# A weight set summed apart, and norm factors carried through DRAM, in a one-core decoder layer

## The chip, the core and the metric

The kernel runs on one core of a Trainium2 chip. The core has a matrix engine (TensorE, PE in the profile), a vector engine (VectorE, DVE), a scalar engine (ScalarE, ACT), GpSimd (POOL) and SyncE (SP), which issues transfers. ACT and POOL issue transfers too. PE writes its results to PSUM; the other data live in SBUF (128 partitions) and in DRAM. Each engine works through its own list of instructions in order, and waits on semaphores for the others.

The metric is the time of one execution in microseconds on the device. The kernel before takes 1294.37 us, the median of three runs (1293.19 to 1296.22).

## What is computed

One hybrid decoder layer for 512 tokens of width 1024, all in float32: a SwiGLU FFN, a mixer with two groups of heads side by side, a cross-attention into a memory of 256 rows, a second FFN, and a final norm. Cut to what the change touches:

```python
def rms_norm(x, w):
    y = x32 * lax.rsqrt(jnp.mean(x32 * x32, axis=-1, keepdims=True) + EPS)
    return y.astype(x.dtype) * w

def swiglu(h, w_in, w_out):                     # D_FF = 2816
    gate, up = jnp.split(h @ w_in, 2, axis=-1)
    return (jax.nn.silu(gate) * up) @ w_out

# mixer, state-space heads: 4 groups of 256 channels
    y = y.reshape(bsz, seqlen, SSD_WIDTH) * jax.nn.silu(z.astype(jnp.float32))
    yg = y.reshape(bsz, seqlen, SSD_GROUPS, SSD_WIDTH // SSD_GROUPS)
    yg = yg * lax.rsqrt(jnp.mean(yg * yg, axis=-1, keepdims=True) + EPS)
    y_ssd = yg.reshape(bsz, seqlen, SSD_WIDTH).astype(h.dtype) * ssd_norm_w
# mixer, differential attention: 8 heads of 128 values
    o = diff_attention(q, k, v, lam, rel_bias)
    o = o * lax.rsqrt(jnp.mean(o * o, axis=-1, keepdims=True) + EPS)
    y_attn = (o.astype(h.dtype) * subln_w * (1.0 - lambda_init)).reshape(bsz, seqlen, DA_WIDTH)
    return jnp.concatenate([y_ssd, y_attn], axis=-1) @ w_out
```

So each of the eight attention heads and each of the four groups needs one factor per token: the inverse root of a mean over 128 or 256 channels.

## The kernel before, in words

Activations lie with channels on the partitions and the 512 tokens along the row. A float32 product is made of three matmuls: both operands are split into a high part (rounded to the type fp32r) and a low part (the rest), and high times high, low times high and high times low are summed in PSUM. A split costs a copy on ACT (`wh`, lines 155 and 1314) and a subtraction on DVE (`wl`, lines 156 and 1316). Weights come in tiles of 128 x 1024 (512 KB).

SP and POOL issue their instructions in the order in which the code is written. On PE, DVE and ACT the order is fixed when the kernel is built. A class `Order` mixes the work: dense products run one after the other, and chains of small steps (heads, groups) are resumed when the PE time already written out passes a due time; a table `W` holds the distances. `behind(...)` ties an instruction behind others on its engine.

**Heads.** `head` (line 768) ends with `po`, the head's output (128 channels x 512 tokens) in PSUM. ACT copies it to `of`; PE transposes it in four blocks (`ptk`), so that tokens lie on partitions; ACT squares the blocks and sums each row (`junk`, `ss`); DVE makes `ev`, POOL raises it to the power -1/2 (`rr`, line 858); DVE multiplies (`on`); PE transposes back (`pot`), and ACT and DVE split the result, with the gain `wsub`, into `yah` and `yal`.

**Groups.** `group` (line 930) ends with two tiles `y`. ACT squares them, DVE adds the squares (`ysq`); PE sums over the channels with a column of ones (`pn`, four float32 matmuls, eight records in the trace); DVE scales (`nv`), POOL takes the power (`ncol`, line 367). `row_of` (line 370) turns the four columns into a row on all partitions: two diagonal matrices (`ndiag`, on POOL for groups 0 to 2) and two PE matmuls with ones (`nrow`). DVE multiplies `y` by its gain and `nrow` (line 1034), and splits.

**The FFN's second product** (`out_blocks`, line 1293) uses a scheme of block sums: `oa`, `oe` and `ob` are PSUM tiles, two each, and weight blocks are added to one another before they are multiplied. The third weight set, S2, multiplies `s24` into `ob`; it is the sum of a set that lies in `wr` and of pieces `more`, added by DVE in place in `wr` (`t2`, line 1362). In the last third of the first FFN (`by_dma`), both parts of S2 are summed behind the two first products, split (`wh`, `wl`), and `ob` starts from a copy of `oa` (line 1422). Two small products `prel`, for the position bias, lie there too.

POOL issues beside this the accumulating transfers (`isum`, `wsum`, 512 KB each) that sum the second FFN's weights in DRAM, long ahead.

Of the kernel before, what the change touches and what calls it, by code (L numbers as in the profile page):

```python
# [38 lines left out]
W |= {"g0": 8.28, "gc": 0.75, "gx": 0.92, "gb": 2.59, "gs": 0.51, "gt": 2.0, "gd": 6.9, "gy": 0.38, "gq": 11.8, "gn": 1.5, "gr": 4.4}  # L39
W |= {"c0": 4.97, "cs": 3.0, "ct": 4.82}  # L40
# [60 lines left out]
def body(tc, a, dbg=None):  # L101
# [38 lines left out]
    last, start, last_sum, recent, newest, newest_mm, first_block, sums_low = [], [], [], [], [], [], [], []  # L140
# [22 lines left out]
    def split(s, src, scale=None, half=False, n=T):  # L163
        if half:
            both = s2(s, R32, (P, 2, T // 2))
            hi, lo = both[:, 0], both[:, 1]
        else:
            hi, lo = s2(s + "h", R32, (P, n)), s2(s + "l", R32, (P, n))
        last[:] = [i.ins for i in split_into(hi, lo, src, scale)]
        return hi, lo  # L170
# [34 lines left out]
    def sums_in_steps(b11, b21, b22, b12, pair=None):  # L205
# [12 lines left out]
        s24 = split("s24", s24)  # L218
        lo, hi = slice(0, H), slice(H, T)
# [149 lines left out]

    def row_of(col, nb, first, second, apart):  # L370
# [71 lines left out]
    def ffn_quads(xs, wq, st, nq, made, places, sums=None, fresh=False, prime=None):  # L442

        for q in range(nq):
# [7 lines left out]
            for i in range(2):  # L452
                row = st.row[:, None, i * H : (i + 1) * H].to_broadcast([P, 2, H])
                V.tensor_tensor(gate[:, 2 * i : 2 * i + 2], halves(gs[i]), row, ALU.mult)  # L454
# [8 lines left out]
    def block_tiles(g, n, tied=False):  # L463
# [12 lines left out]
        def made(th):  # L476
            g.append({})
            if len(g) < n:
                od.spawn(steps(th, g[-1], 2.9), 2.9)
            else:  # L480
                with behind(list(recent) if tied else []):
                    for _ in steps(th, g[-1], 0.0):
                        pass
# [125 lines left out]
    dskh = cp.tile([P, 8], F32, name="dskh")  # L609
    rel_d = dram.tile([8, RW], F32, name="rel_d")  # L610

    def lambdas():
# [15 lines left out]
        V.tensor_scalar(dskh, par[:, C_DSKIP : C_DSKIP + 8], 0.5, None, ALU.mult)  # L628

# [138 lines left out]
    def head(hd, q, kq, bias):  # L768
# [75 lines left out]
        of = s2("of")  # L844
        S.activation(of, po, AF.Copy)
# [24 lines left out]
    def out_attn(hg, o0, o1, prep=False):  # L870
# [3 lines left out]
        for o in range(o0, o1):  # L874
            po = acc("pm")
            yield from proj(po, ws.get(o) or load_w(a["woa"][hg, o], 4 * P), heads)
            V.tensor_tensor(x[o], x[o], po, ALU.add)
# [6 lines left out]
    def silu2(src):  # L884
# [3 lines left out]
        V.scalar_tensor_tensor(th, th, 1.0, src, ALU.add, ALU.mult)  # L888
# [41 lines left out]
    def group(g, bt, ct, xs, zs):  # L930
# [93 lines left out]
        yield W["gq"] + (1.2 if g == 2 else 0.0)  # L1024
        pn = aux("pn", (P, 4))
        for b in range(4):
            mm(pn[:, b : b + 1], sq[0][:, b * P : (b + 1) * P], ones[:, 0:1], True, True)

        rh = inv_rms_cols(pn, 4, 4.0 / (4 * 256), 4.0 * EPS)
        yield W["gn"]  # L1030
        pr = yield from row_of(rh, 4, *((G, G) if g < 3 else (V, V)), W["gr"] - (0.8 if g == 3 else 0.0))
# [261 lines left out]
    def out_blocks(blocks, sums, g, col4, ncol4, each=None, finale=None, clean=True, n=None, by_dma=False):  # L1293
# [14 lines left out]
        def weights(of, part, raw=None, low_behind=()):  # L1308
            if raw is None:
                raw = of(part) if callable(of) else fetch(of, part)  # L1310
            w = raw.shape[1]
            hi = wp.tile([P, w], R32, tag="wh", name=nm("wh"))
            lo = wp.tile([P, w], R32, tag="wl", name=nm("wl"))
            high = S.activation(hi, raw, AF.Copy)  # L1314
            with behind(low_behind):
                low = V.tensor_tensor(lo, raw, hi.bitcast(F32), ALU.subtract)  # L1316
            recent[:] = [high.ins, low.ins]
# [44 lines left out]
        def t2(part):  # L1362
            more = pieces.pop(part) if part in pieces else (fetch(blocks[B22], part),)
            n = t_raw[part].shape[1] // len(more)
            for i, m in enumerate(more):
                V.tensor_tensor(t_raw[part][:, i * n : (i + 1) * n], t_raw[part][:, i * n : (i + 1) * n], m, ALU.add)
            return t_raw[part]

# [7 lines left out]
        def t4(part):  # L1376
            G.dma_start(t_raw[part], blocks[B21][:, part[0] * T : part[1] * T], accum_op=ALU.add)

        later, pieces, asked = {}, {}, {}

        def ask_early():
            for of, make in ((B11, lambda part: fetch(blocks[B11], part)), (S1, t1)):
                asked[of, parts[1]] = make(parts[1])
            for part in parts:
                pieces[part] = [s2("more") for _ in range(*part)]
                for k, m in zip(range(*part), pieces[part]):
                    nc.sync.dma_start(m, blocks[B22][:, k * T : (k + 1) * T])
            for part in parts:
                asked[S3, part] = seventh(part)
# [5 lines left out]
        if here:  # L1395
            seventh = added(blocks[B12], blocks[B22], "gate")
            sums = [early_or(S1, t1), early_or(S3, seventh), t2, lambda part: t_raw[part]]
        ready = [None, None]
        if early:
            ready = [{parts[0]: weights(of, parts[0])} for of in (blocks[B11], sums[0])]  # L1400
            yield
        if by_dma:
            ask_early()
# [15 lines left out]
        third = {part: weights(sums[2], part, low_behind=() if n else sums_low) for n, part in enumerate(parts if by_dma else parts[:1])}  # L1419
        third_split = list(recent) if by_dma else []  # L1420
        for t in range(2):
            S.activation(b_ps[t], a_ps[t], AF.Copy)
        with behind(third_split):
# [8 lines left out]
        for n, _ in enumerate(product(a_ps, b21 if here and not by_dma else blocks[B21], "12")):  # L1432
            if n == 12 and by_dma:
                for part in t_raw:
# [190 lines left out]
```

## Time and profile before

| | |
|---|---|
| median of three runs | 1294.37 us (1293.19 to 1296.22) |
| profiled execution, its own time | 1296.8 us |
| its span | 1295.0 us |
| granted PE clock, mean | 0.996 |
| busy | PE 1282.7, DVE 973.5, ACT 707.2, POOL 116.4 us |
| chain that ended last | PE 98%, DVE 1% |

The profiled execution is one that was watched; its own time lies 2.4 us above the median and is the one that the trace's numbers add up to. "PE busy" counts the time in which a matmul is under way; matmuls overlap one another, so the price of a matmul in a dense stretch is the distance between starts. A row of the timeline gives start, duration, engine, line, operation, tiles (written <- read), shape and count, and in brackets the idle time ahead with what ended it. A row of DMA issues gives the queue, the size, and the median time from issue to landing.

### The profile page before, as it was taken

How to read it: one execution, taken by the hardware profiler on the slowest of the kernel's cores; microseconds unless marked ns; L12 is line 12 of the kernel's file. 1: busy time of each engine (PE TensorE's matmuls, PEld its weight loads, DVE VectorE, ACT ScalarE, POOL GpSimd, SP SyncE). 2: the span in 40 equal slices, each digit the busy share in tenths (PEclk: the TensorE clock that was granted, in tenths of full speed). 3: DMA queues.
4: the chain of work that ended last, by engine and by line, in shares of the span. 5: the costliest groups of instructions: out<-in, count | busy, mean ns of one | idle time of the engine just before them, and what ended most of it. 6: DMA issues, size and time to landing. Idle time of an engine off the chain costs nothing.

```text
span 1295.0 us, 20087 instructions
## 1 busy us (share of the span) xinstructions
PE 1282.7 (99%) x7709; PEld 1124.9 (87%) x7709; DVE 973.5 (75%) x1553; ACT 707.2 (55%) x1203; POOL 116.4 (9%) x145
## 2 busy tenths in 40 slices
PE   9999999999999999999999999999999999999997
PEld 7889998998888788877888888889899999989995
DVE  6988898797875776567778697645678878877886
ACT  7545564565654564346644575435466646555554
POOL 1001010001010011100102011020001000000000
PEclk9999999999999999999999999999999999999998
DMA  9368677889874436653475667593249876666662
GB/s 334 97 175 205 181 204 196 226 200 238 260 242 147 139 66 164 225 165 98 106 206 168 175 161 232 190 231 111 66 131 253 212 228 178 191 189 189 184 198 91
DMA packets 69551, 234.75 MB, mean 181 GB/s; under 512 B 8192, under 2 KB 9696, under 8 KB 69104
## 3 DMA queue, kind: packets, MB, share of 16 engines
q1 hardware_dynamic: 53488, 180.91, 42.5%
q0 software_dynamic: 13168, 45.67, 20.0%
q10 hardware_dynamic: 2800, 6.91, 1.6%
q8 instruction: 60, 0.98, 0.3%
q14 instruction: 35, 0.29, 0.1%
HBM read 231.30 MB, written 48.29 MB: 216 GB/s over the span
## 4 chain that ended last, share of the span: by engine, by line
PE 98%; DVE 1%; ACT 0%; issue 0%; POOLq 0%; POOL 0%; ACTq 0%
PE qb L243 13%; PE pm L146 10%; PE qe L243 8%; PE qa L243 8%; PE pxbc L146 7%; PE ob L1328 7%; PE oa L1328 4%; PE oe L1328 4%; PE pk L146 3%; PE pv L146 3%; PE pq L146 3%; PE pcq L146 3%; PE pz L146 3%; PE pck L146 2%; PE pa L146 2%; PE pcv L146 2%
## 5 line engine op out<-in xcount | busy, mean ns | idle before, releaser
L155 ACT ACTIVATE wh<-wr 128x1024 fp32r<-128x1024 f32 (+1 forms) x245 | 251.5, 1028 | 239.0 <-PE qe L243 29.4
L156 DVE TENSOR_TENSOR wl<-wr,wh 128x1024 fp32r<-128x1024 f32 (+1 forms) x245 | 291.1, 1189 | 78.3 <-ACT wh L155 57.8
L1314 ACT ACTIVATE wh<-wr 128x1024 fp32r<-128x1024 f32 (+1 forms) x78 | 77.1, 988 | 71.3 <-PE ob L1328 19.7
L1316 DVE TENSOR_TENSOR wl<-wr,wh 128x1024 fp32r<-128x1024 f32 (+1 forms) x78 | 87.6, 1131 | 15.1 <-ACT wh L1314 12.9
L790 ACT ACTIVATE ec<-ec,mn 128x512 f32<-128x512 f32 (+3 forms) x64 | 35.4, 554 | 21.9 <-DVE mn L789 21.9
L789 DVE CUSTOM_DVE_ANT_0 ec<-ps,bias 128x512 f32<-128x512 f32 (+3 forms) x64 | 28.1, 487 | 15.4 <-PE ps L146 15.3
L252 POOL DMA_DIRECT2D wr<-in_f2q x11 | 9.7, 881 | 308.8 <-DMA wr<-in_f2q 176.3
L367 POOL TENSOR_TENSOR ncol<-nv,mhalf 128x4 f32<-128x4 f32 (+1 forms) x9 | 10.6, 1179 | 295.3 <-DVE nv L365 295.3
L903 DVE SCALAR_TENSOR_TENSOR conv<-pxbc,par,conv 128x511 f32<-128x511 f32 (+2 forms) x48 | 35.8, 745 | 0.6
L146 PE MATMUL pxbc<-hnl,wh 128*128 128x512 f32 x128 | 35.5, 404 | 0.0
L146 PE MATMUL pxbc<-hnh,wh 128*128 128x512 f32 x128 | 34.7, 398 | 0.0
L146 PE MATMUL pxbc<-hnh,wl 128*128 128x512 f32 x128 | 32.5, 393 | 0.0
L454 DVE TENSOR_TENSOR gate<-qb,row 128x512 f32<-128x512 f32 x19 | 13.2, 692 | 22.1 <-PE qb L243 22.1
L146 PEld LDWEIGHTS pxbc<-hnh,wl 128*128 128x128 f32 x128 | 23.7, 188 | 5.2 <-issue 0.2
L252 POOL DMA_DIRECT2D wr<-in_f1q x16 | 14.0, 874 | 151.9 <-DMA wr<-in_f1q 83.0
L146 PEld LDWEIGHTS pxbc<-hnh,wh 128*128 128x128 f32 x128 | 23.3, 189 | 4.6 <-issue 0.3
L146 PEld LDWEIGHTS pxbc<-hnl,wh 128*128 128x128 f32 x128 | 23.2, 188 | 4.7 <-issue 0.4
L455 ACT ACTIVATE gate<-gate 128x1024 f32<-128x1024 f32 x19 | 20.1, 1056 | 10.9 <-DVE gate L454 10.9
L146 PE MATMUL pv<-wh,hnh 128*128 128x512 f32 x64 | 25.3, 396 | 0.0
L146 PE MATMUL pv<-wh,hnl 128*128 128x512 f32 x64 | 25.2, 393 | 0.0
L155 ACT ACTIVATE s24h<-s 128x512 fp32r<-128x512 f32 x30 | 18.8, 626 | 8.1 <-DVE s L214 8.1
L858 POOL TENSOR_TENSOR rr<-ev,mhalf 128x4 f32<-128x4 f32 x8 | 8.3, 1035 | 162.4 <-DVE ev L856 162.4
(465 smaller groups left out, 3548.1 us busy)
## 6 DMA issues: line engine op xcount, KB each, us to landing
wr<-in_f2q SPq DMA_DIRECT2D x44, 512.0 KB, 4.5
wr<-in_f1q SPq DMA_DIRECT2D x40, 512.0 KB, 4.6
wr<-in_f1b SPq DMA_DIRECT2D x23, 512.0 KB, 7.0
isum<-in_f2q SPq DMA_DIRECT2D x22, 512.0 KB, 5.2
wr<-isum SPq DMA_DIRECT2D x22, 512.0 KB, 6.2
wsum<-in_f2b SPq DMA_DIRECT2D x20, 512.0 KB, 6.1
wr<-wsum SPq DMA_DIRECT2D x20, 512.0 KB, 4.7
wr<-in_f1q POOLq DMA_DIRECT2D x16, 512.0 KB, 7.6
```

The costliest lines, as they stand in the source:

```text
L146: newest_mm[:] = [nc.tensor.matmul(out, w, x, start=start, stop=stop).ins]
L155: S.activation(hi, src, AF.Copy),
L156: V.tensor_tensor(lo, src, hi.bitcast(F32), ALU.subtract),
L243: newest_mm[:] = [nc.tensor.matmul(out, w_[:, wc], xs[kp][which][x_], start=first and j == 0 and f == 0 and kp == 0, stop=j == 2 and kp == ...
L252: last_sum[:] = [G.dma_start(raw, m, accum_op=ALU.add).ins]
L455: S.activation(gate, gate, AF.Silu)
L789: V.tensor_tensor_reduce(out=ec[:, :n], in0=ps[c][:, parts[i]], in1=bias[:, T - n :], scale=0.125, scalar=3e38, op0=ALU.add, op1=ALU.min, ...
L790: S.activation(ec[:, :n], ec[:, :n], AF.Exp, bias=mn, scale=-1.0, accum_out=sm[c][:, i : i + 1])
L903: V.scalar_tensor_tensor(y[:, d:], ps[:, : T - d], par[:, cw + j : cw + j + 1], y[:, d:], ALU.mult, ALU.add)
L1314: high = S.activation(hi, raw, AF.Copy)
L1316: low = V.tensor_tensor(lo, raw, hi.bitcast(F32), ALU.subtract)
L1328: newest_mm[:] = [nc.tensor.matmul(ps, a_[:, ts], b_[:, ws], start=first and k == 0 and j == 0, stop=k == n - 1 and j == 2, skip_group_che ...
```

## The change

It has two parts.

**The third set, apart.** In the last third of the first FFN, S2 is no longer summed into `wr` but into the tiles `more` (`t2_apart`). `third_set` does the adds, the splits and the late loads of the first two sets between the steps that split the last FFN tile; the gate's last multiplication is tied behind them. The fourth set is then accumulated onto the `more` tiles, in four transfers of 256 KB in place of two of 512 KB. `weights` is cut into `high` and `low`.

**Factors through DRAM.** For the heads with `hd % 4 < 3` (six of eight) and for groups 0 to 2, tokens no longer go to the partitions through PE. The squares are split, and two matmuls with ones (`ptok`) sum them over the channels, on all partitions; ACT copies one partition of it as a line, already permuted; a transfer on POOL's queue spreads the line over 128 partitions, four tokens on each (`ssum`); POOL adds the epsilon term and takes the power; a transfer writes the 512 numbers to DRAM as one row (`there`), and another reads this row into all partitions (`far`). DVE multiplies it on, tied behind a late neighbour (`near`). Heads 3 and 7 and group 3 stay as they were.

```diff
+W |= {"hn": 4.2, "fs": 7.0, "fw": 6.0, "fr": 9.0}
...
+    def sums_by_token(sq):
+
+        ps = aux("ptok")
+        with behind(list(newest_mm)):
+            for j in range(2):
+                mm(ps, ones_r, sq[j], j == 0, j == 1)
+        line = s2("line")[0:1]
+        S.activation(line.rearrange("o (p b) -> o b p", b=4), ps[0:1].rearrange("o (b p) -> o b p", b=4), AF.Copy)
+        ss = small("ssum", 4, bufs=2)
+        G.dma_start(ss, line.rearrange("o (p b) -> o p b", b=4))
+        return ss
+
+    def row_by_dram(v):
+
+        col = small("fcol", 4, bufs=2)
+        G.tensor_tensor(col, v, mhalf, ALU.pow)
+        there = dram.tile([4, P], F32, name=nm("there"))
+        G.dma_start(bass.AP(there.tensor, there.offset, [[1, P], [P, 4]]), col)
+        yield W["fw"]
+        row = s2("far")
+        G.dma_start(row, bass.AP(there.tensor, there.offset, [[0, P], [1, 4 * P]]))
+        yield W["fr"]
+        return row
...
             for i in range(2):
                 row = st.row[:, None, i * H : (i + 1) * H].to_broadcast([P, 2, H])
-                V.tensor_tensor(gate[:, 2 * i : 2 * i + 2], halves(gs[i]), row, ALU.mult)
+                with behind(recent[2:] if prime and q == nq - 1 and i else []):
+                    V.tensor_tensor(gate[:, 2 * i : 2 * i + 2], halves(gs[i]), row, ALU.mult)
...
+        if hd % 4 < 3:
+            sq = s2("osq")
+            S.activation(sq, po, AF.Square)
+            S.activation(of, po, AF.Copy, scale=wsub_p)
+            sq = split("osq", sq)
+            yield W["hn"]
+            ss = sums_by_token(sq)
+            ev = small("fev", 4, bufs=2)
+            G.tensor_tensor(ev, sm[0], sm[0], ALU.mult)
+            G.tensor_tensor(ev, ev, eps_p, ALU.mult)
+            yield W["fs"]
+            G.tensor_tensor(ev, ev, ss, ALU.add)
+            row = yield from row_by_dram(ev)
+            with behind(list(near)):
+                V.tensor_tensor(of, of, row, ALU.mult)
+            ya[hd] = split("ya", backwards(of))
+            return
...
+        if g < 3:
+            sq = split("ysq", sq[0])
+            yield W["gq"] + (1.2 if g == 2 else 0.0)
+            ss = sums_by_token(sq)
+            v = small("fev", 4, bufs=2)
+            yield W["fs"]
+            G.tensor_tensor(v, ss, eps_g, ALU.add)
+            pr = yield from row_by_dram(v)
...
         for j in range(2):
             n = 2 * g + j
-            V.scalar_tensor_tensor(yz[j], yz[j], par[:, C_SSD + n : C_SSD + n + 1], pr, ALU.mult, ALU.mult)
+            gain = par[:, C_SSD + n : C_SSD + n + 1] if g == 3 else gain_p[:, n : n + 1]
+            with behind(list(near) if g < 3 else []):
+                V.scalar_tensor_tensor(yz[j], yz[j], gain, pr, ALU.mult, ALU.mult)
...
+        def t2_apart(part):
+            for i, m in enumerate(pieces[part]):
+                recent.append(V.tensor_tensor(m, t_raw[part][:, i * T : (i + 1) * T], m, ALU.add).ins)
...
         def ask_early():
+            ask_pieces(parts[0])
             for of, make in ((B11, lambda part: fetch(blocks[B11], part)), (S1, t1)):
                 asked[of, parts[1]] = make(parts[1])
...
+            ask_pieces(parts[1])
+            t2_apart(parts[0])
+            between.append(third_set)
+
+        def third_set():
+            ready[0][parts[1]] = weights(None, parts[1], asked.pop((B11, parts[1])), first_block)
+            with behind(first_block[:1]):
+                w = high(parts[0], pieces[parts[0]])
+            copied_behind[:] = recent
+            with behind(first_block):
+                ready[1][parts[1]] = weights(None, parts[1], asked.pop((S1, parts[1])))
+            with behind(sums_low + recent[1:]):
+                t2_apart(parts[1])
+            third[parts[0]] = low(w)
```

Constants for the new path (`wsub_p`, `gain_p`, `eps_p`, `eps_g`) are made at the start.

How the lists move is shown at three places. The first is the end of the last FFN third on DVE; `more` are the pieces of S2, `wr` the set they are added to. Before:

```order
L454 TENSOR_TENSOR gate_3380<-qb_3135,row_412 128x512
L1316 TENSOR_TENSOR wl_3377<-wr_3373,wh_3376 128x1024
...
L156 TENSOR_TENSOR s31l_3397<-s_597_3391,s31h_3396 128x512
L156 TENSOR_TENSOR s24l_3401<-s_598_3392,s24h_3400 128x512
L156 TENSOR_TENSOR gl_3405<-th_3381,gh_3404 128x512
L1366 TENSOR_TENSOR wr_3373<-wr_3373,more_3413 128x512
L1366 TENSOR_TENSOR wr_3373<-wr_3373,more_3414 128x512
L1366 TENSOR_TENSOR wr_3410<-wr_3410,more_3417 128x512
L1366 TENSOR_TENSOR wr_3410<-wr_3410,more_3418 128x512
```

With the change:

```order
L1443 TENSOR_TENSOR more_3387<-wr_3380,more_3387 128x512
L1443 TENSOR_TENSOR more_3388<-wr_3380,more_3388 128x512
L1392 TENSOR_TENSOR wl_3384<-wr_3380,wh_3383 128x1024
L482 TENSOR_TENSOR gate_3402<-qb_3142,row_415 128x512
...
L157 TENSOR_TENSOR s31l_3419<-s_603_3413,s31h_3418 128x512
L1443 TENSOR_TENSOR more_3396<-wr_3393,more_3396 128x512
L1443 TENSOR_TENSOR more_3397<-wr_3393,more_3397 128x512
L1392 TENSOR_TENSOR wl_3427<-more_3387,wh_3426 128x512
L1392 TENSOR_TENSOR wl_3427<-more_3388,wh_3426 128x512
L157 TENSOR_TENSOR s24l_3439<-s_604_3414,s24h_3438 128x512
L1392 TENSOR_TENSOR wl_3512<-more_3396,wh_3511 128x512
L1392 TENSOR_TENSOR wl_3512<-more_3397,wh_3511 128x512
```

The first part's two adds have gone from behind `gl` to ahead of the last `gate`, and the second part's from there to behind `s31l`.

The second place is the end of head 0 on PE, inside a `pq` product (queries of a later head). Before:

```order
L146 MATMUL pq_4554<-hnl_3919,wh_4557 128x512
L150 MATMUL ptk_4582<-ident,of_4576 128x128 x4
L146 MATMUL pq_4554<-hnl_3947,wh_4557 128x512
L146 MATMUL pq_4554<-hnl_3969,wh_4557 128x512
L146 MATMUL pq_4554<-hnl_3999,wh_4557 128x512
```

With the change:

```order
L147 MATMUL pq_4571<-hnl_4044,wh_4574 128x512
L147 MATMUL ptok_4613<-osqh_4597,ones_r 128x512
L147 MATMUL pq_4571<-hnl_4064,wh_4574 128x512
L147 MATMUL pq_4571<-hnh_3887,wl_4575 128x512
L147 MATMUL ptok_4613<-osql_4598,ones_r 128x512
```

Two matmuls of 512 columns stand near the place where four transposes stood, and the four of `pot` further on are gone.

The third place is group 2, whose last step falls beside the memory's value product (`pcv`, weights `wcv`). On ACT with the change (`ptok` is the group's sum, `btk` the next group's):

```order
L156 ACTIVATE wh_8129<-wr_8127 128x1024
L942 ACTIVATE th_1680_7955<-conv_7931 128x512
L942 ACTIVATE th_1681_7962<-pz_7922 128x512
L156 ACTIVATE wh_8212<-wr_8210 128x1024
L380 ACTIVATE line_8024<-ptok_8021 1x4x128
L1016 ACTIVATE btk_8033<-pbt_8029 128x384
```

On POOL with the change:

```order
L382 DMA ssum_8026<-line_8024 128x1x4
L1355 DMA wsum_288<-in_f2b 128x1024
L1085 TENSOR_TENSOR fev_8028<-ssum_8026,eps_all 128x4
L388 TENSOR_TENSOR fcol_8122<-fev_8028,mhalf 128x4
L390 DMA there_8124<-fcol_8122 128x4x1
L393 DMA far_8167<-there_8124 128x512
L1355 DMA wsum_289<-wsum_287 128x1024 x2
```

And on DVE, from the last multiplication of `gate` to that of `th`, which PE's next `py` reads:

```order
L1050 TENSOR_TENSOR gate_7796<-gate_7796,cbm_7993 128x512
L1099 SCALAR_TENSOR_TENSOR y_7799<-y_7799,gain_p,far_8167 128x512
L157 TENSOR_TENSOR wl_8260<-wr_8257,wh_8259 128x1024
L1065 SCALAR_TENSOR_TENSOR y_8186<-th_1674_7915,dskh,py_8096 128x512
L157 TENSOR_TENSOR wl_8301<-wr_8298,wh_8300 128x1024
L1066 TENSOR_TENSOR y_8186<-y_8186,e_1722_8097 128x384
L1074 TENSOR_TENSOR y_8186<-y_8186,th_1681_7962 128x512
L1050 TENSOR_TENSOR th_7893<-th_7893,cbm_7993 128x512
L1063 SCALAR_TENSOR_TENSOR e_1737_8191<-pf_8267,e_1737_8191 128x384
L157 TENSOR_TENSOR ysl_8248<-y_7799,ysh_8247 128x512
L1050 TENSOR_TENSOR th_7893<-th_7893,cbm_7993 128x512
```

In the old list both multiplications of `y` stood ahead of the row of `gate` that heads this list; now they stand behind it. Between the group's `ssum` and its `fev` POOL issues an accumulate of 512 KB; the two that followed it now follow `far`.

More of the change, by code (lines that the diff above doesn't have):

```diff
@@ L138, in dump @@
             nc.sync.dma_start(dbg[name], t.bitcast(F32) if t.dtype == R32 else t)
[L140 removed]
+    last, start, last_sum, recent, newest, newest_mm, first_block, sums_low, second_high, between, near = ([] for _ in range(11))
     V, S, G = nc.vector, nc.scalar, nc.gpsimd
@@ L1418, in out_blocks @@
         u2 = []
[L1419 to L1423, printed above, removed]
+        if not by_dma:
+            third[parts[0]] = weights(sums[2], parts[0], low_behind=sums_low)
+        with behind(copied_behind + (second_high if by_dma else [])):
+            copied = [S.activation(b_ps[t], a_ps[t], AF.Copy).ins for t in range(2)]
+        if by_dma:
+            with behind(copied):
+                third[parts[1]] = weights(None, parts[1], pieces[parts[1]])
+        with behind(list(recent) if by_dma else []):
             for t in range(2):
```

88 lines of the change are left out of this document (54 added, 34 removed).

## The prediction

> **What bounds the kernel now.** I read the page's busy shares first, then the view of waits of TensorE (PE), then the chain of waits, then the timeline of each place that the change touches.
>
> ```profile
> PE 1282.7 (99%) x7709; PEld 1124.9 (87%) x7709; DVE 973.5 (75%) x1553; ACT 707.2 (55%) x1203; POOL 116.4 (9%) x145
> PE 98%; DVE 1%; ACT 0%; issue 0%; POOLq 0%; POOL 0%; ACTq 0%
> PE ob L1328 <- ACT wh L1314: 1.1, 1, 1.1
> 321.31 5.44 PE oa L1328 x24
> 313.97 7.33 PE ob L1328 x24
> ```
>
> PE is busy 99% of the span, and the chain that ends last is PE for 98%. Twenty-four matmuls of 512 columns take 5.44 us, so one takes 0.227 us start to start. The third row is the one PE wait behind the start, 1.1 us at `ob`; the last shows 24 matmuls behind it that took 7.33 us. So there are two ways to shorten the kernel: fewer PE instructions, and that one stall. VectorE (DVE, 75%), ScalarE (ACT, 55%) and GpSimd (POOL, 9%) count only where they make PE wait.
>
> **First part, the third weight set.** The place is the end of the last third of the first FFN.
>
> ```profile
> 311.48 2.49 DVE L1366 TENSOR_TENSOR wr<-wr,more 128x512 f32<-128x512 f32 x4
> 311.82 1.03 PE L146 MATMUL prel<-hot,rel_sb 32*8 32x256 f32 x4
> 312.86 2.27 ACT L1314 ACTIVATE wh<-wr 128x1024 fp32r<-128x1024 f32 x2 [1.14 <-DVE wr L1366]
> 313.97 1.45 PE L1328 MATMUL ob<-wh,s24h 128*128 128x512 f32 x4 [1.13 <-ACT wh L1314]
> 300.94 0.69 DVE L454 TENSOR_TENSOR gate<-qb,row 128x512 f32<-128x512 f32 x1 [2.80 <-PE qb L243]
> 313.90:318.30 4.40, 4.33 (x12) 3.42 (x13) 4.40 (x7) 3.46 (x7) 2.49 (x3) 0.61 1.00 282
> ```
>
> DVE adds `wr<-wr,more` late, ACT's high copy waits 1.14 us for it, and PE waits 1.13 us for the copy. The last row (busy of PE, PEld, DVE, ACT, POOL, then granted clock, DMA share, GB/s) shows what follows: the clock is 0.61 in these 4.4 us. So the stall costs 1.13 + (7.33 - 5.44 = 1.89) = 3.02 us.
>
> The change puts the adds of the first part into DVE's idle 2.80 us ahead of `gate`, and its high copy on ACT (1.03 us by the row of 77.1 us for 78 would be 0.99) ahead of `s31h`. What is late next is the second part: its adds (two of 0.62), the low copies of the first (two of about 0.65) and `s24l` stand in DVE's order behind `s31l`, which starts at about 309.5; ACT copies `ob` from 310.7 to 311.7. PE leaves the old `oe` at 311.8, and one of the two `prel` products now stands ahead of `ob`, so `ob` finds its inputs some 0.3 to 0.8 us early. I take the whole 3.02; bounds: 1.13 if only the wait goes and the clock drops anyway, 0 if the stall only moves. The `prel` work stays. The accumulates into the third set become four of 256 KB for two of 512 KB, with the same bytes on the same queue; their sums are read by the last of the products, several passes of 5.44 us later, and cost nothing.
>
> **Second part, six heads and three groups.** What leaves PE:
>
> ```profile
> L150 PE MATMUL ptk<-ident,of x32: 272/273/329, 417.3 to 644.4; 128*128 128x128 f32 x32
> L150 PE MATMUL pot<-ident,on x32: 270/272/273, 423.5 to 651.6; 128*128 128x128 f32 x32
> 630.68 0.71 PE L146 MATMUL pxbc<-hnl,wh 128*128 128x512 f32 x2
> 631.22 0.60 PE L150 MATMUL pot<-ident,on 128*128 128x128 f32 x4
> 631.58 0.71 PE L146 MATMUL pxbc<-hnh,wl 128*128 128x512 f32 x2
> 540.48 1.30 PE L146 MATMUL pv<-wl,hnh 128*128 128x512 f32 x5
> 541.62 0.95 PE L146 MATMUL pn<-ones,ysq 128*128 128x1 f32 x8
> 543.22 0.40 PE L146 MATMUL pv<-wh,hnh 128*128 128x512 f32 x1
> 548.92 0.39 PE L146 MATMUL pv<-wh,hnl 128*128 128x512 f32 x1
> 549.14 0.62 PE L146 MATMUL nrow<-ndiag,ones_r 128*128 128x512 f32 x2
> 549.61 0.40 PE L146 MATMUL pv<-wh,hnh 128*128 128x512 f32 x1
> ```
>
> Durations of matmuls overlap, so I price a group by start to start. From 630.68 to 631.58 are 0.90 us, two pxbc are 0.453, so four transposes cost 0.447. The same at the twelve groups of the six heads gives 0.31 to 0.57 each, together 4.98. From 540.48 to 543.22 are 2.74 us, eight pv are 1.814, so `pn` costs 0.93 (0.79 to 0.93 at the three groups, together 2.60). The two-matmul `nrow` costs 0.69 - 0.227 = 0.46 (0.46 to 0.68, together 1.61). What comes: nine `ptok` pairs of the same shape as `nrow`, 9 x 0.47 = 4.22. Net 4.98 + 2.60 + 1.61 - 4.22 = 4.97 us. PE is dense around all these rows, so this is time on the path.
>
> With the first part, PE loses 3.02 + 4.97 = **8.0 us**.
>
> DVE and ACT: a head loses four squares with their accumulator reads, `on`, two `ev`; it gains one square, a high and a low part, a product and a copied line. That is about even, beside PE, and so is the group's part (`nv`, `ch` and `cl` against a low part and the line). The few constants at the start lie ahead of work that waits for its first load. What costs is a longer road for the factor: line (ACT), spread by transfer, pow (POOL), to DRAM, broadcast back.
>
> ```profile
> L414 ACT ACTIVATE row<-nrow x4: 365/598/602, 28.7 to 975.8; 128x512 f32<-128x512 f32 x3, 128x256 f32<-128x256 f32 x1
> cum_d<-ct_sb POOLq DMA_DIRECT2D x1, 32.0 KB, 2.5
> 348.41 0.90 POOL L1290 DMA_DIRECT2D isum<-in_f2q  x1
> ii<-in_ii POOLq DMA_DIRECT2D x1, 2.0 KB, 7.1
> gain<-in_final POOLq DMA_DIRECT2D x2, 256.0 KB, 4.6
> wsum<-in_f2b POOLq DMA_DIRECT2D x1, 512.0 KB, 6.1
> wsum<-wsum POOLq DMA_DIRECT2D x2, 512.0 KB, 11.1
> L858 POOL TENSOR_TENSOR rr<-ev,mhalf 128x4 f32<-128x4 f32 x8 | 8.3, 1035 | 162.4 <-DVE ev L856 162.4
> 442.99 0.68 DVE L156 TENSOR_TENSOR kl<-pk,kh 128x512 fp32r<-128x512 f32 x1
> 629.15 1.55 PE L146 MATMUL pxbc<-hnl,wh 128*128 128x512 f32 x6
> 648.19 0.68 DVE L888 SCALAR_TENSOR_TENSOR th<-th,conv 128x512 f32<-128x512 f32 x1
> 923.30 2.50 SPq L250 DMA_DIRECT2D wr<-isum  x2
> ```
>
> The line takes 0.6. The two small transfers (2 KB each) lie between 2.5 (`cum_d`, the one POOL transfer to DRAM, with nothing ahead of it) and 7.1 (`ii`, of 2 KB, issued 0.6 us behind the 512 KB accumulate of 348.41). I take 2.5 where nothing stands ahead. Add and pow take 1.3 (`rr` 1.04 and a short one), the broadcast 4.6. The sum is 0.6 + 2.5 + 1.3 + 2.5 + 4.6 = 11.5 us. Behind an accumulate of 512 KB in POOL's queue a transfer lands only after it, as `ii` did; alone that one lands 6.1 us behind its issue, two together 11.1. So a road with one ahead takes some 16 us. By the order, the multiplication stands 19 to 25 us behind its `ptok` at eight of the nine places: the first from 417.3, in the place of `ptk`, to behind `kl` of 442.99, the shortest, head 6, from 629.5 to behind the `th` of 648.19. That is enough. POOL also waits in its queue for each sum and each `there`, and so the accumulates behind come 5 to 13 us later. They sum weights of the second FFN, read first at 923.3, over 100 us behind; without that cover each would cost its delay.
>
> The ninth is group 2, whose rows are these.
>
> ```profile
> 765.18 1.06 ACT L155 ACTIVATE wh<-wr 128x1024 fp32r<-128x1024 f32 x1 [2.67 <-PE pm L146]
> 772.70 0.68 DVE L995 TENSOR_TENSOR gate<-gate,cbm 128x512 f32<-128x512 f32 x1
> 774.69 1.22 DVE L156 TENSOR_TENSOR wl<-wr,wh 128x1024 fp32r<-128x1024 f32 x1
> 775.83 0.74 DVE L1010 SCALAR_TENSOR_TENSOR y<-th,dskh,py 128x512 f32<-128x512 f32 x1
> 781.56 0.69 DVE L995 TENSOR_TENSOR th<-th,cbm 128x512 f32<-128x512 f32 x1
> 783.32 1.09 PE L146 MATMUL py<-th,xdt 128*64 128x128 f32 x16
> ```
>
> In ACT's order `line` stands behind the `wh` of the first row, which waits for PE. So it runs from 766.2 to 766.8, on the old time line, and the sums land at 769.3. POOL issues a `wsum` accumulate just behind them, at about 767.6, which lands at 773.7. Add and pow are done at 770.6; `there`, issued then, lands at 773.9 behind the accumulate, and `far`, issued then, at 778.5. DVE has done `gate` (773.4) and the `wl` that now stands ahead (1.22) by about 774.8, and waits 3.7 us. Behind it on DVE stand the product (0.74), two `wl` (2.44), `y` (0.74 + 0.55 + 0.69), `e` (0.55), a low part (0.69) and two `th` (1.38), together 7.8: the last `th` is done at 786.3. PE's `py` needs it; five matmuls (1.13) now stand ahead of `py`, so at 784.45. PE stalls 1.8 us. The stall at `ob` was 1.13 us and was followed by 1.89 us of slow clock, so I add 1.9: **3.7 us** go back. Bounds: 0 (no stall) and 5.5 (far 1.8 later).
>
> The Trainium skill (TensorE: Matmul & The Clock Gate, Part 1, "What's actually happening") has the clock halved after an idle window of about 3.4 us; here it fell behind 1.13 us, so the measurement decides. By that page the new stall would cost 1.8 alone, and the time would be 1288.2, inside the forecast's own range.
>
> Sum: 8.0 - 3.7 = 4.3 us. The profiled execution took 1296.8, with a span of 1295.0 and 1.8 around it, and becomes 1292.5; the median of the runs is 1294.37, 2.4 below the profiled one, and becomes **1290.1**.
>
> **The rivals.**
>
> No stall at group 2. It vanishes when `far` lands before 784.45 - 7.8 = 776.65, 1.85 earlier than reckoned. For it: the other two `wsum` accumulates, which shared the DMA engines with that one in the old order, now stand behind `far`. Against it: 6.1 is that very transfer's own row, and it was the first of the three. Then 1294.4 - 8.0 = 1286.4.
>
> Small transfers as slow as `ii` without anything ahead, the case that ends slower. `there` writes 512 single numbers of 4 bytes, and the spread writes 128 pieces of 16 bytes; no row shows such shapes alone, and the only row of 2 KB has 7.1. At group 2 the sums land at 773.9, pow is done at 775.2, `there` lands at 782.3, `far` at 786.9: 8.4 later than reckoned. The stall is 10.2, with the slow clock 12.1, the sum -4.1: 1298.5, and heads with 19 us to spare would begin to be late too. It turns into a loss when the stall passes 6.1, so when `far` lands 4.3 us later than reckoned. Against it: `ii` had an accumulate ahead, which accounts for its 7.1. The Trainium skill (DMA: Bandwidth & Descriptors, "Rules for kernel authors") speaks for it: a last dimension that isn't contiguous is lowered to one descriptor per element, and should be rearranged. No run here shows that yet. With that page's 10.5 ns for a packet ("Bandwidth"), `there` would take an estimated 5.4 us, and the time would be 1292.3.
>
> One more place is late. Group 1's eight `mem` transfers now stand behind its `there` and `far` on POOL, with about 1 us to spare; head 6 has `far` behind an accumulate, with 2 to 4 us. One more stall like the one at `ob` costs about 3: 1293.1.
>
> The stall at `ob` stays, since the second part's adds are late instead: 3.0 come back, 1293.1.
>
> The removed groups were covered by something else, so that PE gains nothing from them: 1294.4 - 3.0 = 1291.4, less what group 2 takes, 1295.1. Against it: the 0.227 us holds on both sides of every group.
>
> **How the numbers follow.** Forecast 0.37, no stall at group 2 0.33, one more place 0.12, slow small transfers 0.08, the old stall stays 0.07, gain covered 0.03. Runs of this kernel can tell about 0.2% from no change, 2.6 us: faster is below 1291.8, slower above 1297.0. The forecast's own range, 1288.3 to 1292.5, lies below 1291.8 for nearly nine tenths of its share. Faster: 0.33 + 0.33 and 0.05 from the cases near 1293 = 0.71. Slower: 0.05, most of the slow transfers. The rest, 0.24, is the same. The range reaches from 1285.6 (the no-stall case with 0.8 of price error) to 1294.6, which takes in one more late place.
>
> **What would show it.** In the profile after: no wait of PE at the first `ob` of that third, and 5.4 us for its 24 matmuls in the chain; PE busy about 5 us less; in the waits, DVE at the group product waiting for the DMA `far` only in group 2, by 3 to 4 us, and PE `py` waiting for DVE `th` there by about 2, with a granted clock below 1 behind it; the small transfers at about 2.5 us in the list of DMA issues. Wrong are my numbers if `there` shows 5 us or more, if more products wait for `far`, or if `ob` still waits.

## The result, and the profile after

The changed kernel takes 1331.9 us (median of 4, 1331.51 to 1332.27) against 1294.88 for the kernel before (median of 4, one run more than at the prediction): a ratio of 1.0284, with a 95% interval of 1.0272 to 1.0296. It is 37 us slower. I had forecast 1290.1, and the slower rival that I named ended at 1298.5.

The page's first rows after (span; busy time of each engine), PE's view of waits (engine, line, what was waited for: us in total, times, longest), three rows of DVE's, and three rows of the DMA issues (queue, count, KB each, median us to landing):

```profile
span 1330.2 us, 20037 instructions
PE 1287.7 (97%) x7649; PEld 1125.2 (85%) x7649; DVE 975.1 (73%) x1555; ACT 714.7 (54%) x1183; POOL 135.8 (10%) x183
PE pcv L147 <- DVE wl L157: 9.4, 1, 9.4
PE pt L151 <- DVE ec L838: 7.5, 1, 7.5
PE pxt L151 <- DVE th L943: 6.6, 1, 6.6
PE py L147 <- DVE gate L1050: 4.0, 1, 4.0
PE py L147 <- DVE th L1050: 2.8, 1, 2.8
PE pf L147 <- DVE st L1033: 1.4, 2, 0.9
DVE of L896 <- DMA far<-there: 22.0, 5, 8.7
DVE y L1099 <- DMA far<-there: 14.6, 1, 14.6
DVE hm L161 <- ACT hm L160: 11.9, 4, 10.2
ssum<-line POOLq DMA_DIRECT2D x9, 2.0 KB, 2.0
there<-fcol POOLq DMA_DIRECT2D x9, 2.0 KB, 10.2
far<-there POOLq DMA_DIRECT2D x9, 256.0 KB, 5.9
```

The last rows point to the cause. `ssum` and `there` move the same 2 KB, in 2.0 and in 10.2 us. DVE waits 36.6 us for `far`, and PE, which had one wait of 1.1 us behind the start, has waits of 9.4, 7.5, 6.6, 4.0 and 2.8 us and small ones, 33 us in all. None stands at `ob`. The span of this profile is 35.2 us longer than that of before: PE is idle for 30.2 us more and busy for 5.0 us more, though some 5 us of its work were taken out.

Not every wait comes from `far`. Those at `gate` and `pf` stand at group 1. There DVE waits 10.2 us, through ACT's `hm`, for the memory's transfers `mem`, which POOL issues behind `there` and `far`. So the rival of one more late place came true here; in contig16, below, the waits at this place are gone.

POOL's timeline at head 4 (start, duration) shows one such transfer with no accumulate issued in the 35 us ahead of it, and the windows of two stretches (busy us of PE, PEld, DVE, ACT, POOL, then the granted clock, DMA share, GB/s) show what the waits bring with them:

```profile
598.96 0.84 POOL L390 DMA_DIRECT2D there<-fcol  x1 [0.30 <-POOL fcol L388]
609.76 0.56 POOL L393 DMA_DIRECT2D far<-there  x1 [9.97 <-DVE ec L838]
311.00:322.00 11.00, 11.00 (x49) 8.50 (x48) 8.86 (x14) 7.88 (x14) 3.37 (x4) 1.00 1.00 222
800.00:840.00 40.00, 27.84 (x124) 22.18 (x123) 20.89 (x30) 12.05 (x20) 5.89 (x7) 0.79 0.74 181
```

`far` can't be issued for 10.8 us. (The row names `ec` as what released it. But `there` lands 10.2 us behind its issue, at 609.2, and at all nine places `far` follows 0.5 to 0.7 us behind that landing, whatever the row names.) The third row is the end of the third FFN third: PE busy throughout, clock 1.00, so the stall there is gone. The last is group 2: 12 us idle in 40, and a clock of 0.79.

### The profile page after: what moved, and what is told of

It reads as the page before. It is cut to its first block, busy times and chain, and to the rows that moved or that the text cites. A ratio compares the mean times of both kernels' runs of the same rounds, so it can differ in the third digit from the quotient of the medians.

```text
span 1330.2 us, 20037 instructions
## 1 busy us (share of the span) xinstructions
PE 1287.7 (97%) x7649; PEld 1125.2 (85%) x7649; DVE 975.1 (73%) x1555; ACT 714.7 (54%) x1183; POOL 135.8 (10%) x183
## 5 line engine op out<-in xcount | busy, mean ns | idle before, releaser
L156 ACT ACTIVATE wh<-wr 128x1024 fp32r<-128x1024 f32 (+1 forms) x245 | 251.0, 1028 | 222.0 <-PE qe L246 31.6
L157 DVE TENSOR_TENSOR wl<-wr,wh 128x1024 fp32r<-128x1024 f32 (+1 forms) x245 | 290.1, 1185 | 92.3 <-ACT wh L156 68.2
L1383 ACT ACTIVATE wh<-wr 128x1024 fp32r<-128x1024 f32 (+1 forms) x74 | 72.8, 984 | 66.8 <-PE ob L1403 19.5
L1392 DVE TENSOR_TENSOR wl<-wr,wh 128x1024 fp32r<-128x1024 f32 (+1 forms) x74 | 82.6, 1125 | 11.7 <-ACT wh L1383 11.2
L382 POOL DMA_DIRECT2D ssum<-line x9 | 6.0, 665 | 220.4 <-ACT line L380 161.9
L483 ACT ACTIVATE gate<-gate 128x1024 f32<-128x1024 f32 x19 | 20.1, 1057 | 10.8 <-DVE gate L482 10.8
L156 ACT ACTIVATE s24h<-s 128x512 fp32r<-128x512 f32 x30 | 18.8, 626 | 10.3 <-DVE s L216 10.3
L156 ACT ACTIVATE s31h<-s 128x512 fp32r<-128x512 f32 x30 | 18.8, 625 | 8.7 <-DVE s L214 4.8
```

What stands on the lines that cost most here:

```text
L156: S.activation(hi, src, AF.Copy),
L157: V.tensor_tensor(lo, src, hi.bitcast(F32), ALU.subtract),
L483: S.activation(gate, gate, AF.Silu)
L1383: recent[:] = [S.activation(hi[:, i * n : (i + 1) * n], r, AF.Copy).ins for i, r in enumerate(raw)]
L1392: recent.append(V.tensor_tensor(lo[:, ns], r, hi[:, ns].bitcast(F32), ALU.subtract).ins)
```

## Experiments

My theory after the result: each `there` writes 512 single numbers of 4 bytes, and this takes 10 us in place of 2.5; the factors come late, DVE waits for them in order, and PE waits for what stands behind on DVE; at group 1 the transfers behind `there` on POOL's queue are late in the same way. The rivals: POOL's queue with its accumulates is slow, or a write to DRAM as such, or the third weight set does the harm.

**contig16**: the same bytes as 128 pieces of 16 bytes.

```diff
-        G.dma_start(bass.AP(there.tensor, there.offset, [[1, P], [P, 4]]), col)
+        G.dma_start(bass.AP(there.tensor, there.offset, [[4, P], [1, 4]]), col)
...
-        return row
+        return row.rearrange("q (p b) -> q b p", b=4)
```

> The transfer `there` writes the same 2 KB, but each partition's four numbers lie side by side: 128 pieces of 16 bytes in place of 512 of 4; DVE reads the row `far` in the permuted order. Nothing else moves. Theory (the 512 single numbers are what takes `there` 9.3 to 11.9 us): it lands in about 2 to 2.5 us, as the spread of 128 pieces of 16 bytes did (2.0), the waits of DVE for `far` go but for group 2, and the time is about 1290 (1286 to 1293). Rival (POOL's queue with its accumulates, or a write to DRAM as such, is what is slow): `there` stays at 9 to 10 us and the time above 1325.

Measured: 1297.5 us (1295.6 to 1298.17, 11 runs), a ratio of 1.0023 (1.0014 to 1.0032) to before. That is 34 us less than the changed kernel. The rows of `there`, of PE's waits, of group 2, of a stretch in it (read as the windows above) and of the accumulate:

```profile
there<-fcol POOLq DMA_DIRECT2D x9, 2.0 KB, 2.8
PE pcv L147 <- DVE wl L157: 3.1, 1, 3.1
PE py L147 <- DVE th L1051: 2.8, 1, 2.8
PE pt L151 <- DVE ec L838: 0.3, 1, 0.3
760.59 0.88 POOL L1357 DMA_DIRECT2D wsum<-in_f2b  x1
765.51 0.65 POOL L390 DMA_DIRECT2D there<-fcol  x1 [0.30 <-POOL fcol L388]
772.67 0.57 POOL L393 DMA_DIRECT2D far<-there  x1 [6.51 <-PE pcv L147]
776.71 1.13 DVE L1101 SCALAR_TENSOR_TENSOR y<-y,gain_p,far 128x512 f32<-128x512 f32 x1 [7.89 <-DMA far<-there]
777.00:790.00 13.00, 8.21 (x33) 6.21 (x34) 12.26 (x16) 5.10 (x7) 0.00 (x0) 0.61 0.88 223
wsum<-in_f2b POOLq DMA_DIRECT2D x1, 512.0 KB, 10.1
```

The way in which `there` is written is the loss. The waits at the other eight places shrink to one of 0.3 us and one of 0.2. Group 2 keeps a stall, at the place that I had named and larger than reckoned: the accumulate ahead takes 10.1 us (last row, the DMA issues of that stretch), DVE waits 7.9.

**pieces8**: 256 pieces of 8 bytes.

```diff
-        G.dma_start(bass.AP(there.tensor, there.offset, [[1, P], [P, 4]]), col)
+        G.dma_start(bass.AP(there.tensor, there.offset, [[2, P], [2 * P, 2], [1, 2]]), col.rearrange("p (h l) -> p h l", l=2))
```

> The same 2 KB of `there` as 256 pieces of 8 bytes. The factors come back in another order of the tokens, so their values are for the wrong tokens; the work is the same. Theory (time by the piece): 128 pieces of 16 bytes take about 2 us and 512 of 4 about 10, so 256 take 4.5 to 5, and the time lies between 1290 and 1310. Rival (any piece below some size is equally slow): about 10 us and 1330.

Measured: 1297.9 us; the median of `there` is 4.7 us. This lies between 2.8 and 10.2, as the theory of the pieces had it.

**third_only** and **factors_only**: each part of the change alone, by leaving out the other part's hunks of the diff.

> The kernel before with only the third weight set summed apart. Theory: the stall of 1.13 us at `ob` and its 1.89 us of slow clock go, 3.0 us, 1291.9. Rival (the third set is part of the loss, or its stall moves elsewhere): no gain, 1294.9 or more.

> The kernel before with only the factors of six heads and three groups through DRAM. Theory (the whole loss is here): 1331.9 + 3.0 = 1334.9. Rival (part of the loss comes from the third set): clearly below 1331.9.

Measured: third_only 1294.04 against 1293.98 for before on the same chip, a ratio of 0.9998 (0.9989 to 1.0007): no gain that can be told. factors_only 1320.5 (1319.22 to 1322.49), a ratio of 1.0204 (1.019 to 1.0218): slower alone, but 11.4 us less than both parts together. Its PE waits sum to 24 us against 33. The same transfers are late in both; at head 5 the factor comes about 4 us later behind its sums with both parts. Why the one order brings them later by so much was not settled.

**before_again**: the kernel before, profiled once more, because its stall is gone in third_only and yet nothing is won.

> The kernel before, profiled once more. The third weight set summed apart alone changed the median by 0.06 us, though the stall that it removes cost 3.0 us in the one profile of before, whose span was 1295.0. Theory (that profile shows more of this stall than the usual execution): a span near 1292, a granted clock of 0.998, and at the first `ob` of the third FFN third a wait well below 1.13 us, or 24 matmuls behind it in 5.44 us. Rival (the stall is always there, and what the third set gains there it loses elsewhere): 1.1 us of wait and 7.3 us for the 24 matmuls, as before.

Measured: 1295.2 us, a span of 1293.4, a clock of 0.998. The timeline at `oe` and `ob`, and the chain at `ob`:

```profile
310.18 0.73 PE L1328 MATMUL oe<-wh,s31l 128*128 128x512 f32 x2 [0.84 <-DVE s31l L156]
313.92 0.96 PE L1328 MATMUL ob<-wh,s24h 128*128 128x512 f32 x3 [1.13 <-ACT wh L1314]
313.92 5.74 PE ob L1328 x24
```

The wait is there again, 1.13 us. The 24 matmuls behind it take 5.74 us, not 7.33, so the slow clock of 1.89 us was 0.30 here. But PE also waits 0.84 us for `s31l` ahead of it, which the first profile does not show. So the whole stretch has to be measured, from the start of the block `oa<-wh,g11h` ahead of both waits (306.21 in before) to that of `oa<-wh,gh` behind the 24 matmuls (321.14). It takes PE 12.4 us in third_only. With the old set it takes 14.9 in before, 14.4 in before_again, 13.0 in factors_only, and 15.4 in g2old_no_third, an experiment below. The old set's price at this place was thus 2.6, 2.0, 0.6 and 3.1 us: it changes from one execution to the next. The two executions with the slow clock, the first and the last, lie 2.4 and 2.7 us above the medians of their kernels.

**contig_g2old**: 16-byte pieces, and group 2 as in the kernel before.

```diff
-        if g < 3:
+        if g < 2:
             sq = split("ysq", sq[0])
```

> `there` in 128 pieces of 16 bytes, and group 2 as it was in the kernel before (sums and factors through PE). Theory (group 2's late factor is all that is left of the loss, and the other eight places give their PE time): its stalls of 3.1 and 2.8 us go, PE saves 2.16 + 2 x 0.91 = 3.97 us against before, so 1290.0. Rival (the PE time of the removed groups does not come back in full): 1292 to 1294.

Measured: **1288.66 us** (1288.28 to 1288.93, 5 runs), a ratio of 0.9949 (0.9936 to 0.9962) to before. It is faster than both kernels. What the eight places give is read from two PE rows each, the start of `pq` before the first place and of `pcv` behind the last, of third_only:

```profile
367.20 1.09 PE L146 MATMUL pq<-hnh,wh 128*128 128x512 f32 x4
762.90 0.84 PE L146 MATMUL pcv<-wh,hm 128*128 128x512 f32 x3
```

and of contig_g2old, with its PE waits:

```profile
366.95 1.32 PE L147 MATMUL pq<-hnh,wh 128*128 128x512 f32 x5
759.45 0.84 PE L147 MATMUL pcv<-wh,hm 128*128 128x512 f32 x3
PE pxt L151 <- DVE th L944: 0.4, 1, 0.4
PE pt L151 <- DVE ec L838: 0.3, 1, 0.3
```

The distance is 395.70 in the one and 392.50 in the other: 3.20 us less, with 0.7 us of new waits in it. So the work removed is 3.9, against 3.97 priced.

**contig_g2late**: 16-byte pieces, group 2 through DRAM, its multiplication tied behind the second masked product of `th`.

```diff
             pr = yield from row_by_dram(v)
+            if g == 2:
+                yield 7.0
+                near[:] = masked
```

> `there` in 128 pieces of 16 bytes, and group 2's multiplication tied behind the second masked product of group 3's last head pair, ten instructions later on DVE; all else as in the first of these kernels. Theory (the stall comes from DVE waiting in order ahead of what PE needs next): both waits of PE in group 2 go, PE saves 4.97 us, so 1289.0. Rival (the factor is then late for the next step as well): no better than 1293.

Measured: 1290.5 us (1288.6 to 1290.99), a ratio of 0.9962 (0.9949 to 0.9976). Both stalls of group 2 are gone. One wait of 1.4 us has come behind them:

```profile
PE pm L147 <- DVE cvl L161: 1.4, 1, 1.4
```

So the order on DVE was what passed the late factor on to PE. Expected was 1289.0. The new wait does not explain the 1.5 us more by itself: the profiled execution has it, and took 1288.6. What the other executions lose was not found.

**there_act**: single numbers again, issued on ACT's queue.

```diff
-        G.dma_start(bass.AP(there.tensor, there.offset, [[1, P], [P, 4]]), col)
+        S.dma_start(bass.AP(there.tensor, there.offset, [[1, P], [P, 4]]), col)
```

> As the changed kernel, 512 single numbers, but `there` is issued on ACT's queue in place of POOL's. Theory (the pieces are slow in the DMA engines): about 10 us again. Rival (POOL's way of making the pieces is slow): 2 to 4 us on ACT's queue. The time of the run says little, since ACT now waits for POOL's power.

Measured: a time of 1319.9, and

```profile
there<-fcol ACTq DMA_DIRECT2D x9, 2.0 KB, 10.3
```

The way through POOL's queue is not the cause.

**contig_hold**: 16-byte pieces, and the accumulate between group 2's `ssum` and `there` held back.

```diff
+            held[:] = [g] if g == 2 else []
             ss = sums_by_token(sq)
...
+                while held:
+                    yield 1.0
                 to, _, more = jobs[n - LEAD]
                 G.dma_start(to, more, accum_op=ALU.add, max_dma_last_dim=4 * D)
```

> The changed kernel with `there` in 128 pieces of 16 bytes, and in group 2 the accumulate of 512 KB that POOL issues between `ssum` and `there` is held back until `far` is issued. DVE's order stays. Theory (in group 2 that accumulate holds `there`, 6.6 us from issue to landing against 1.7 where nothing stands ahead): `there` lands in about 2, `far` some 4.7 us earlier, DVE waits about 3 in place of 7.9 us, PE's waits of 3.1 and 2.8 us shrink to 1.2 in all, and the time is about 1291. Rival (the loads on SP's queue slow `there` whatever stands ahead): `there` at 5 us or more, and about 1297.

Measured: 1295.2 us (1293.36 to 1297.57), a ratio of 1.0006 (0.9997 to 1.0015). Group 2 in its timeline, and PE's waits:

```profile
765.28 0.64 POOL L390 DMA_DIRECT2D there<-fcol  x1 [0.30 <-POOL fcol L388]
768.21 0.56 POOL L393 DMA_DIRECT2D far<-there  x1 [2.29 <-issue]
773.57 1.15 DVE L1103 SCALAR_TENSOR_TENSOR y<-y,gain_p,far 128x512 f32<-128x512 f32 x1 [5.00 <-DMA far<-there]
PE py L147 <- DVE th L1052: 3.8, 1, 3.8
PE qb L246 <- DVE c L313: 1.2, 1, 1.2
```

The accumulate did hold `there`: `far` is issued 2.9 us behind it, not 7.2. But DVE still waits 5.0 us, and PE 3.8 and 0.2 in place of 5.9, not the 1.2 expected; `far`, from its issue to DVE's start, now takes 5.4 (773.57 - 768.21) against 4.0 (776.71 - 772.67). The wait at `qb` is new; it lies in the second FFN, where SP's list of loads now runs in another order, but whether that is its reason was not tried. So some 2 us are won where 6.5 were expected. The mechanism holds, the size does not.

**g2old_no_third**: contig_g2old without the third set.

> As contig_g2old, the fastest so far (1288.66), but with the third weight set summed in place as before. Theory (the stall at `ob` costs about 1.1 us of waiting and 0.3 of slow clock in the usual execution, not 3.0): 1290.1. Rival (the third set gains nothing): 1288.7. Rival (it gains the 3.0 that I predicted): 1291.7.

Measured: 1289.78 us (1288.31 to 1292.45, 7 runs), 1.1 above contig_g2old. The two ran on different chips; by their ratios to before, 0.9967 (0.9956 to 0.9978) and 0.9949 (0.9936 to 0.9962), the difference is 2.3 us. So a gain of the third set is likely here, where third_only showed none; but the two intervals overlap, and whether it is 1.4 or 3.0 can't be told. The 1.1 us wait at `ob` is in this profile again, with the slow clock behind it.

**spaced**: 16-byte pieces, and ahead of each `there` a transfer of the 512 single numbers, 64 bytes apart, that nobody reads.

```diff
+        wide = dram.tile([4, 16 * P], F32, name=nm("wide"))
+        G.dma_start(bass.AP(wide.tensor, wide.offset, [[16, P], [16 * P, 4]]), col)
         there = dram.tile([4, P], F32, name=nm("there"))
```

> `there` in 128 pieces of 16 bytes, and ahead of it, at each of the nine places, one more transfer `wide`, whose result nobody reads: the same 512 single numbers to DRAM, but 64 bytes apart. Theory (time by the piece): `wide` takes about 10 us. Rival (neighbouring numbers of 4 bytes get in each other's way in DRAM): 2 to 4 us. The time of the run only says how much was added.

Measured: a time of 1298.1, and a median of 3.1 us for `wide` (2.3 to 6.1). Here my theory fell: the same count of pieces, and a third of the time. The rival took its place, and four more runs tested it: **apart4, apart8, apart16, apart32**, the same dead transfer with its numbers 4, 8, 16 and 32 bytes apart (1, 2, 4 and 8 for 16 in the diff above).

> As `spaced`, but the 512 numbers of the dead transfer `wide` lie 4 bytes apart, as `there` of the changed kernel had them. Theory (numbers of 4 bytes that lie near each other in DRAM and are written as pieces of their own hold each other up): about 10 us, and the time near that of the changed kernel. Rival (a transfer that nobody reads is quick, and near or far makes no difference): 2 to 4 us.

> `wide` with its numbers 8 bytes apart. Theory (the cost goes by how many pieces fall into one stretch of DRAM, and 256 pieces of 8 bytes side by side took 3.3 to 6.4 us): 4 to 6 us. Rival (only exact neighbours): 2 to 3 us.

> `wide` with its numbers 16 bytes apart. Theory: 128 pieces of 16 bytes side by side took 1.7 to 2.3 us in quiet places, so about 3 us. Rival (the count of pieces matters as well): 4 us or more.

> `wide` with its numbers 32 bytes apart. Theory: 2.3 us in quiet places, as with 64 bytes. Rival (64 bytes are needed): 3 us or more.

The row of `wide` in the DMA issues of apart4, then of apart8, of apart16, of apart32, and of spaced:

```profile
wide<-fcol POOLq DMA_DIRECT2D x9, 2.0 KB, 9.9
```

```profile
wide<-fcol POOLq DMA_DIRECT2D x9, 2.0 KB, 5.0
```

```profile
wide<-fcol POOLq DMA_DIRECT2D x9, 2.0 KB, 3.7
```

```profile
wide<-fcol POOLq DMA_DIRECT2D x9, 2.0 KB, 3.1
```

```profile
wide<-fcol POOLq DMA_DIRECT2D x9, 2.0 KB, 3.1
```

The times of the four are 1324.8, 1301.2, 1299.7 and 1298.8 us. Packed at 4 bytes it is slow whether it is read or not, and each doubling of the distance brings the time down until 32 bytes. So 512 single numbers as such are cheap here, and the price is that they lie close together in DRAM. What in the memory or the DMA engines makes close pieces wait for one another, no run here shows.

## Why the prediction was wrong

- **`there` at 2.5 us** is the step that failed. I took it from `cum_d`, a transfer of 32 KB, with the bounds 2.5 and 7.1 from two rows of other shapes. It took 9.3 to 11.9 at all nine places, outside both bounds. The rival of slow small transfers had the right operation and its shape, but I gave it 0.08, because `ii`'s 7.1 was explained by the accumulate ahead of it. That explanation said nothing on the shape, which no row showed. The rival was not right throughout: it had 7.1 for the spread `ssum` too, which took 2.0. The Trainium skill's rule (DMA: Bandwidth & Descriptors, "Rules for kernel authors") to rearrange so that the last dimension is contiguous was the right warning, and contig16 bears it out: 34 us. The 5.4 us that I worked out from that page's 10.5 ns for a packet was half of the 10.2 measured, and the reason was another: with the same 512 pieces 64 bytes apart it is 3.1.
- **"That is enough"** for eight of nine places rested on a road of 11.5 to 16 us. With `there` at 10.2 it is some 8 us longer, and the 19 to 25 us no longer suffice. DVE waits for `far` at six of the nine. Even the slow rival priced only group 2, and the heads brought waits of 7.5 and 6.6 us. POOL's list carries the lateness on: with `there` late, POOL issues `far`, an accumulate and head 5's `ssum` within 1.2 us of one another (starts 609.76, 610.31 and 610.89), and that `ssum` lands 8.3 us behind its issue in place of 2.0. At group 1 it makes `mem` late, the place that I had given 1 us to spare and a chance of 0.12.
- **Group 2** was the right place, by the mechanism that I gave (line behind `wh`, accumulate ahead, DVE's order in front of PE). The sizes were off: the accumulate took 10.1 us, not 6.1; DVE waited 7.9 where I had 3.7; and PE stalled twice (3.1 at a `wl` that my sum passed over, 2.8 at `th`). Why the accumulate took longer was not tried; SP's loads of `wos` were in flight beside it, and they took 6.7 us there against 3.5 in contig_hold, where it is held back. contig16, which has all that I had priced but for the shape of `there`, gave 3.5 us more than before, not 4.3 less. So with `there` in time the forecast would still have failed, above its range. The stretch from the first `pcv` to the first `pm` with `ysh`, with two rows of PE's timeline from third_only and two from contig16:

```profile
762.90 0.84 PE L146 MATMUL pcv<-wh,hm 128*128 128x512 f32 x3
790.59 0.62 PE L146 MATMUL pm<-ysh,wh 128*128 128x512 f32 x2
```

```profile
759.07 1.08 PE L147 MATMUL pcv<-wh,hm 128*128 128x512 f32 x4
795.24 1.52 PE L147 MATMUL pm<-ysh,wh 128*128 128x512 f32 x6
```

It is 27.7 us in the one and 36.2 in the other: 8.5 us, in the place of my 3.7. That is some 5 of the 7.8 us by which contig16 missed the forecast gain (4.3 + 3.5); what the third set, next, did not give is most of the rest.
- **The third set at 3.02 us** was a reading of one execution. The wait (0.9 to 1.13 us in every profile of the old set) was usual, the slow clock behind it (1.89) came in two of four. The stretch cost 2.6, 2.0, 0.6 and 3.1 us in those four. The gain is about 1.1 us by the medians of two kernels on different chips, 2.3 by their ratios, and not to be told from none by those of third_only: its size stays open. I had noted that the profiled time lay 2.4 above the median, and yet took a stall's whole price from it.
- **The slow clock after a stall** came as the row at `ob` had said: 0.61 in the 13 us of contig16's group 2, with waits of 3.1 and 2.8. As a price for every stall it is uncertain, since it came in two of the four profiles with the old set. The Trainium skill (TensorE: Matmul & The Clock Gate, Part 1) gives an idle window of about 3.4 us; waits of about 1.1 us with and without a slow stretch behind them are what these runs show. (The 1288.2 that I gave by that page lies just below my own range, which begins at 1288.3, and not inside it.)
- **PE's own sum**, 4.97 us less for groups and heads, held: 3.9 of 3.97 at the eight places of contig_g2old. The price of the removed groups was right, and worth 5 us against a road that cost some 40.

## What to carry to other kernels

Before a factor is sent through DRAM, look at what lies next to each single number there. Let each partition write its numbers side by side, and put the permutation into the engine that reads the result: 128 pieces of 16 bytes took 2.8 us where 512 neighbouring numbers took 10.2. A transfer that no row of the profile shows in its own shape has no price from rows of another shape, so its bound must be wide; and a late transfer is paid for again in every list behind it that goes in order, here POOL's and DVE's. And when a single profile lies above the median of the runs, take a stall's price only from what a second profile shows again.

## What the runs showed of the hardware that I had not expected

- Single numbers of 4 bytes written to DRAM take 9.9, 5.0, 3.7, 3.1 and 3.1 us for 512 of them at distances of 4, 8, 16, 32 and 64 bytes, from POOL's queue; on ACT's the packed ones take 10.3 as well.
- Others in flight beside such a transfer are slower. The loads of `wos` that SP issued around group 2 took 12.5 us in the changed kernel and 6.7 with the 16-byte pieces (the DMA issues of the two stretches). They took 9.6 in factors_only and 8.4 in apart4, which have packed numbers too, and 6.4 to 7.7 in pieces8, contig_g2late, spaced and the three other apart runs, with the same accumulate ahead:

```profile
wr<-in_wos SPq DMA_DIRECT2D x2, 512.0 KB, 12.5
```

```profile
wr<-in_wos SPq DMA_DIRECT2D x2, 512.0 KB, 6.7
```

- Copying one partition of 512 numbers in permuted order (`line`) took 1.07 us on ACT, not the 0.6 of a plain copy (the row of the changed kernel, then two of contig16). Reading the permuted `far` made DVE's product 1.07 us in place of 0.69, and that of the groups 1.13 in place of 0.74:

```profile
L380 ACT ACTIVATE line<-ptok x9: 1042/1065/1086, 416.4 to 786.7; 1x512 f32<-1x512 f32 x9
```

```profile
L897 DVE TENSOR_TENSOR of<-of,far x6: 1057/1070/1104, 440.4 to 645.4; 128x512 f32<-128x512 f32 x6
L1101 DVE SCALAR_TENSOR_TENSOR y<-y,gain_p,far x6: 1117/1131/1159, 562.4 to 784.2; 128x512 f32<-128x512 f32 x6
```
